# Two transformer blocks on one core: the first layer's modulation by single tiles of features

## The chip, the cores and the metric

The kernel runs as one program on one core of a Trainium2 chip, in float32. The metric is the device time of one launch in microseconds (us), the median of several runs. TensorE (PE in the profile) multiplies matrices; its weight loads have a row of their own (PEld). VectorE (DVE), ScalarE (ACT) and GpSimd (POOL) do the elementwise work, and SyncE (SP) issues the transfers. Each engine works through its own list in order, and waits on semaphores for the others.

## The reference

Two blocks one after the other; 256 latent tokens `x` and 256 context tokens `ctx`, 1024 features. The change lies in the head of the first block's first layer: the modulation and the norm ahead of the first projections.

```python
def first_block(x, c, ctx, c_ctx, w_ada, b_ada, g_norm, w_in, ...):
    silu_c = jax.nn.silu(c)
    silu_cc = jax.nn.silu(c_ctx)
    for l in range(DEPTH):
        mod_lat = silu_c @ w_ada[l] + b_ada[l]
        mod_ctx = silu_cc @ w_ada[l] + b_ada[l]
        x, ctx = _layer(x, ctx, mod_lat, mod_ctx, ...)
    return _rms_norm(x, g_final)
```

In `_layer` the modulation is cut into shift, scale and gate (1024 each). The layer's input is rms_norm(x) * g_norm * (1 + scale) + shift, with one shift and scale for the latent and one for the context tokens, and `w_in` projects it to queries, keys, values and gates. A second layer, and a second block of attention and feed-forward layers, follow.

## The kernel before

Features lie on the 128 partitions: `x[:, k, :]` is tile k of 8, with 512 tokens along it (latent, then context). Products of float32 data are made of three products in the matmul's own rounded format: data and weights are each split into a high part (a cast, on ACT) and a low part (the difference, on DVE or POOL), and `mm` is called for high x high, low x high and high x low. `w_split` splits a piece of weights of 128 x 1024.

The head of layer 0 (`first_layer` with `l == 0`, lines 359 to 426) runs like this. SP loads `x` in four transfers, then for q = 0 to 3 four pieces of `w_ada` (512 columns of shift and scale, that is two tiles of features with their four rows each) and one piece of `w_in_t1`, the weights of the first projection, two tiles of features in a piece. Every transfer here is 512 KB. `Squares` sums the squares of `x` over the features: seven tiles are added up, the columns of that sum and of the last tile's squares are taken by small matmuls (line 100, `tr<-ones,t`), and `rstd` makes the row statistic (`sqm`, then `rcx` by a power on POOL, line 287).

The rest is written as steps, whose order is the string `PLAN["start"]`; `issue_after` keeps each step behind the last matmul so far, and a scheduler sets the final order on each engine from its own estimates of times.

- `d`: one piece of `w_ada` into the sums of the modulation (`ada_mm`, line 184). The sum over 1024 is cut into four quarters, each in its own 32 columns of the array; a piece holds two of the eight k.
- `s`, `b`: the statistic, and its broadcast to all partitions (`rb`, named `tg` in the trace); then all eight tiles of `x` are multiplied by it in place, four on DVE and four on POOL (line 401, `xres`).
- `l`: the modulation of two tiles of features (`ada_rows`): the sums are copied out (line 196, `adarows`), transposed, added up over the quarters on DVE (line 201) with bias and gain (202, 205); then `normed` for both tiles: scale and shift on ACT (line 338), the high part `xyh` (340) and the low part `xyl` (341) on DVE.
- `w`: the split of a piece of `w_in_t1`, the low part on POOL (the table `POOL_LO` holds all four of `t01`).
- `t`: 6 products of one tile of 128 tokens with the two tiles of features of a piece (tiles of PSUM `pv` and `sc`).

Behind it come chunk 3 of the projections (`w_in_t3`, 96 products into `acc` and `sc`), chunk 0, and the attention, which has the steps `d04` and `d05` among its own: the gates' part of the modulation, eight pieces of `w_ada` that are loaded into the four buffers `st`.

Of the kernel before, what the change touches and what calls it, by code (L numbers as in the profile page):

```python
# [10 lines left out]
F32 = mybir.dt.float32  # L11
# [17 lines left out]
def _cols(*spans):  # L29
# [10 lines left out]
# shift 8, scale 8, gate 8  # L40
# [4 lines left out]
# orders of the steps whose results meet only at the end (see the tables `steps`)  # L45
PLAN = {
# [10 lines left out]
# pieces of weights whose low parts are worked out by GpSimd (see the keys given to `fetch`)  # L57
# [5 lines left out]
# tile 0, 1: latent tokens; 2, 3: context tokens  # L63
# [5 lines left out]
def tile_two_blocks(ctx: ExitStack, tc: tile.TileContext, A, out, dbg=None):  # L69
# [104 lines left out]
    # ------------------------------------------------------------------ first block  # L174
# [33 lines left out]
    def ada_src(l, j, i):  # L208
        return A["w_ada"][l, j, :, i * 1024:(i + 1) * 1024]
# [7 lines left out]
    bada = const("b_ada")       # [128, l, 24]  # L217
    gnorm = const("g_norm")
    c2 = const("cvec")
# [28 lines left out]
    class Squares:  # L248
        """sum over the features of squares, a tile of 128 features at a time; a column of sums for each tile of tokens"""
# [14 lines left out]
        def add(self, ap, scale=1.0):  # L264
# [10 lines left out]
            if self.k == KT - 1:        # all but the last tile: ahead of it  # L275
# [4 lines left out]
        def mean(self, dst):  # L280
            """mean of the squares + eps"""
# [8 lines left out]
    def inv_rows(rr, cols):  # L290
        """columns of heads -> rows of 1 / x, a pair of heads in the two halves of the partitions, a pair after the other"""
# [14 lines left out]
    mod_rows = {}       # what is left of the next layer's shifts, scales and gates, and behind which tile  # L306

    def first_layer(l, ncx, x, rc):
        """ncx: context tokens are updated (layer 0) or only read (layer 1)"""
# [8 lines left out]
        # ---- norm  # L318
# [8 lines left out]
        def normed(k, t, r=None):  # L327
            xf = T2()
            if r is not None:
                t1, t = t, T2()  # L330
            # the first tile by halves: the products wait for it
            for hs in (((1,), (0,)) if l and k == 0 else ((0, 1),)):
                s = slice(hs[0] * 256, hs[-1] * 256 + 256)
                if r is not None:
                    V.tensor_tensor(t[:, s], t1[:, s], r[:, s], op=OP.mult)
# [20 lines left out]
        if l == 0:  # L356
# [32 lines left out]
            def st_d(i):  # L389
                q, i = divmod(i, 4)  # L390
                if i == 0:
                    acc[q] = bank("acc")
# [1087 lines left out]
```

## Time and profile before

| | |
|---|---|
| median of 3 runs | 1162.22 us (1160.79, 1162.22, 1164.43) |
| span of the profiled execution | 1164.8 us |
| PE busy over the span | 1110.9 us, 95% |
| DVE, ACT, POOL busy | 765.8, 596.9, 311.7 us |
| HBM read | 164.41 MB, 142 GB/s over the span |

The profiled execution's only time is its span, from the first instruction to the last; it lies 2.6 us above the median and 0.4 above the highest run. A matmul's end is modelled in the trace, so PE's durations overlap; what a matmul costs is read from the distance between two starts. Float32 matmuls (line 100 with `s` or `ones`, line 156) leave two records each, the others one. A timeline row gives the start, the duration, engine and line, what is written from what, the count, and in brackets the engine's idle time ahead of it and what ended that.

### The profile page before, as it was taken

To read this page: it belongs to the slowest core of one execution; us is meant where nothing else is said; L and a number is where in the kernel's file an instruction comes from. 1 tells how busy PE (TensorE), PEld (TensorE's weight loads), DVE (VectorE), ACT (ScalarE), POOL (GpSimd) and SP (SyncE) were. 2 spreads that over 40 slices of the span, in tenths; PEclk is the share of its full clock that TensorE was granted. 3 is DMA by queue.
4 is the path that set the end of the run, shared out by engine and by line. 5 is a ranking of instruction groups with operands and counts; after the bars stand their busy time and mean duration, and the time that the engine had idled before them with its cause. 6 is when DMAs were issued, how large, how long until landed. Compare 5 with 4: busy or idle time off the path is not lost. (4 is left out here: it accounts for less than half of the span.)

```text
span 1164.8 us, 20350 instructions
## 1 busy us (share of the span) xinstructions
PE 1110.9 (95%) x7762; PEld 963.1 (83%) x7762; DVE 765.8 (66%) x1497; ACT 596.9 (51%) x1154; POOL 311.7 (27%) x290
## 2 busy tenths in 40 slices
PE   5899998999899899998999999999999989999997
PEld 2586777687686789887776899999998789999996
DVE  3465555585646666778676777776557877777653
ACT  3435643533434366465456565555447856555541
POOL 3452311131212544424313312221032241222100
PEclk9999998999899899999999999999999999999998
DMA  9523501433742324214443255555644325555561
GB/s 347 200 66 125 177 28 39 142 130 123 259 153 73 101 91 146 74 69 143 162 153 118 82 175 195 184 183 179 182 145 150 135 71 181 185 183 189 175 186 47
DMA packets 52608, 167.29 MB, mean 144 GB/s; under 512 B 6816, under 2 KB 10400, under 8 KB 52512
## 3 DMA queue, kind: packets, MB, share of 16 engines
q1 hardware_dynamic: 52512, 166.01, 42.8%
q8 instruction: 61, 1.00, 0.3%
q14 instruction: 35, 0.29, 0.1%
HBM read 164.41 MB, written 1.05 MB: 142 GB/s over the span
## 5 line engine op out<-in xcount | busy, mean ns | idle before, releaser
L131 ACT CAST wh<-st 128x1024 fp32r<-128x1024 f32 (+4 forms) x272 | 268.5, 992 | 208.9 <-PE acc L100 116.3
L132 DVE TENSOR_TENSOR wl<-st,wh 128x1024 fp32r<-128x1024 f32 (+4 forms) x207 | 244.5, 1183 | 113.3 <-ACT wh L131 108.9
L132 POOL TENSOR_TENSOR wl<-st,wh 128x1024 fp32r<-128x1024 f32 (+4 forms) x65 | 150.9, 2332 | 285.1 <-ACT wh L131 264.5
L100 PE MATMUL acc<-xyh,wh 128*128 128x512 f32 (+1 forms) x320 | 112.5, 352 | 4.3 <-DVE xres L892 2.3
L100 PE MATMUL acc<-xyl,wh 128*128 128x512 f32 (+1 forms) x320 | 111.5, 351 | 2.6 <-DVE xyl L132 2.6
L100 PE MATMUL acc<-xyh,wl 128*128 128x512 f32 (+1 forms) x320 | 111.4, 349 | 0.0
L100 PE MATMUL acc<-wh,xyh 128*128 128x512 f32 (+1 forms) x256 | 97.6, 382 | 6.4 <-DVE t L474 3.3
L100 PE MATMUL sc<-hh,wl 128*128 128x256 f32 x352 | 99.0, 281 | 0.0
L100 PE MATMUL sc<-hl,wh 128*128 128x256 f32 x352 | 99.0, 281 | 0.0
L100 PE MATMUL acc<-hl,wh 128*128 128x256 f32 x352 | 99.0, 281 | 0.0
L100 PE MATMUL acc<-ah,wh 128*128 128x256 f32 x352 | 99.0, 281 | 0.0
L100 PE MATMUL acc<-al,wh 128*128 128x256 f32 x352 | 99.0, 281 | 0.0
L100 PE MATMUL acc<-ah,wl 128*128 128x256 f32 x352 | 98.9, 281 | 0.0
L100 PE MATMUL sc<-hh,wh 128*128 128x256 f32 x352 | 98.9, 281 | 0.0
L100 PE MATMUL acc<-hh,wh 128*128 128x256 f32 x352 | 98.8, 281 | 0.0
L100 PE MATMUL acc<-hh,wl 128*128 128x256 f32 x352 | 98.8, 281 | 0.0
L100 PE MATMUL acc<-wh,xyl 128*128 128x512 f32 (+1 forms) x256 | 96.0, 375 | 0.0
L100 PE MATMUL acc<-wl,xyh 128*128 128x512 f32 (+1 forms) x256 | 95.3, 376 | 0.0
L100 PEld LDWEIGHTS acc<-xyh,wh 128*128 128x128 f32 x320 | 62.2, 194 | 13.5 <-issue 2.8
L100 PEld LDWEIGHTS acc<-xyl,wh 128*128 128x128 f32 x320 | 62.0, 194 | 10.8 <-DVE xyl L132 3.1
L100 PEld LDWEIGHTS acc<-xyh,wl 128*128 128x128 f32 x320 | 62.0, 194 | 7.6
L100 PEld LDWEIGHTS sc<-hl,wh 128*128 128x128 f32 x352 | 66.4, 189 | 0.0
(458 smaller groups left out, 2746.2 us busy)
## 6 DMA issues: line engine op xcount, KB each, us to landing
st<-w_gu SPq DMA_DIRECT2D x88, 512.0 KB, 3.8
st<-w_dn SPq DMA_DIRECT2D x32, 512.0 KB, 3.5
st<-w_in_t SPq DMA_DIRECT2D x24, 512.0 KB, 3.9
st<-w_in_f SPq DMA_DIRECT2D x24, 512.0 KB, 4.7
st<-a_w_qkv SPq DMA_DIRECT2D x24, 512.0 KB, 3.4
st<-w_ada SPq DMA_DIRECT2D x20, 512.0 KB, 3.9
st<-w_out SPq DMA_DIRECT2D x16, 512.0 KB, 4.4
st<-w_dn SPq DMA_DIRECT2D x16, 384.0 KB, 3.3
```

Source lines behind the costliest of these rows:

```text
L100: last_mm[0] = PE.matmul(o, lhsT, rhs, start=start, stop=stop).ins
L131: S.copy(hi, src)
L132: (lo_eng or V).tensor_tensor(lo, src, hi.bitcast(F32), op=OP.subtract)
```

## The change

The modulation of shift and scale is worked out a tile of features at a time. On the host the weights of shift and scale of layer 0 become an array of their own, `w_ada0`, one block of 256 columns (scale and shift of one tile) for each tile. Its two halves of 512 KB are loaded in the order tile 0, piece 0 of `w_in_t1`, tiles 1 and 2, piece 1, tiles 3 and 4, and so on; bytes and number of transfers stay the same. `st_d` makes the sums of one tile: in each half it runs the four quarters side by side, with 256 columns. `st_b` only broadcasts the statistic; the eight multiplications of `x` in place are gone, and the statistic is applied in `st_l` together with the gain: `u = x * gm * rb` (DVE, line 427), the high part as `u + shift` rounded by ACT (428), the low part as `(u + shift) - high` (DVE, 429), in halves of 256 tokens, context first. `bada1` (the bias plus one) is made at the start on POOL. All four splits of `w_in_t1` go to DVE. `st_t` takes one tile of features with all four tiles of tokens, 12 products. The order of steps is new: the column sums and the statistic stand first, and the modulation of the next tile stands ahead of a tile's products.

```diff
-    "start": "d s d d d w b d d d l d l d t t t d w t t d d d l t d d w t t t d t l t t w t t t t",
+    "start": "s d0 b l0 d1 w0 l1 d2 t0 l2 d3 w1 t1 l3 d4 t2 l4 d5 w2 t3 l5 d6 t4 l6 d7 w3 t5 l7 t6 t7",
...
+    bada1 = consts.tile([128, 8], F32, name="bada1")
+    G.tensor_scalar(bada1.rearrange("p (a b) -> p a b", b=2),
+                    bada[:, 0, 0:16].rearrange("p (a b) -> p a b", b=4)[:, :, 0:2], 1.0, None, op0=OP.add)
...
             for q in range(4):
-                tiles = ada_tiles(q)
-                for i, t in enumerate(tiles):
-                    with after(last_load[0]):
-                        load(t, ada_src(0, q, i))
-                wa.append(tiles)
-                with after(last_load[0]):
-                    w1.append(w_load(A["w_in_t1"][0, :, q * n1:(q + 1) * n1]))
+                load_a(2 * q)
+                load_w(q)
+                load_a(2 * q + 1)
...
-            def st_d(i):
-                q, i = divmod(i, 4)
-                if i == 0:
-                    acc[q] = bank("acc")
-                ada_mm(acc[q], i, wa[q][i])
+            def st_d(k):
+                ps = acc[k] = bank("acc")
+                for i in range(2):
+                    for u in range(4):
+                        r = slice(u * 32, u * 32 + 32)
+                        mm(ps[r, :256], s32[:, 4 * i + u, :], wa[k][i][:, u * 256:(u + 1) * 256], i == 0, i == 1)
...
             def st_b():
-                S.copy(rb, bcast4(acc["r"]))
-                for k in range(KT):
-                    (V if k < 4 else G).tensor_tensor(x[:, k, :], x[:, k, :], rb, op=OP.mult)
-
-            def st_l(q):
-                ada_rows(0, q, acc[q])
-                for k in (2 * q, 2 * q + 1):
-                    normed(k, x[:, k, :])
+                pb = bcast4(acc["r"])
+                S.copy(rb, pb)
+
+            def st_l(k):
+                rows = consts.tile([128, 512], F32, name="adarows", bufs=1)[:, :256]
+                S.copy(rows, acc[k][:, :256])
...
+                V.reduce_sum(m, pt[:, :256].rearrange("p (i u r) -> p i r u", u=4, r=32)[:, :, 0:2, :], axis=AX.X)
+                V.tensor_scalar(gm[:, k, :], mod[:, ks, :], bada1[:, k:k + 1], gnorm[:, l, k:k + 1], op0=OP.add, op1=OP.mult)
...
+                for i in (1, 0):
+                    c = slice(i * 256, i * 256 + 256)
+                    V.scalar_tensor_tensor(u[:, c], x[:, k, c], gm[:, k, i:i + 1], rb[:, c], op0=OP.mult, op1=OP.mult)
+                    S.activation(xnh[:, k, c], u[:, c], AF.Identity, bias=sh[:, i:i + 1])
+                    V.scalar_tensor_tensor(xnl[:, k, c], u[:, c], sh[:, i:i + 1], xnh[:, k, c].bitcast(F32),
+                                           op0=OP.add, op1=OP.subtract)
 
             def st_w(q):
-                w1[q] = w_split(w1[q], str(q) in POOL_LO.get("t01", ""))
+                w1[q] = w_split(w1[q], False)
```

On TensorE, from the statistic to the first product of the projections (`pv` from `xyh`), before the change (`kh` holds a piece of `w_ada` here, `wh_217` a split piece of `w_in_t1`):

```order
L156 MATMUL tr_221<-c_ident_64,rcx_203 128x128 x4
L100 MATMUL acc_235<-wh_123,s32_84 32x512 x2
L100 MATMUL acc_235<-wl_124,s32_84 32x512 x2
L100 MATMUL acc_235<-wh_125,s32_84 32x512 x2
L156 MATMUL tr_244<-c_ident_64,adarows_242 128x128 x4
L100 MATMUL acc_235<-wl_126,s32_84 32x512 x2
L156 MATMUL tr_266<-c_ident_64,adarows_264 128x128 x4
L100 MATMUL acc_284<-kh_133,s32_84 32x512 x2
L100 MATMUL pv_287<-wh_217,xyh_108 128x512
```

and with the change, from the column sums on:

```order
L100 MATMUL tr_192<-ones_66,t2_172 128x2 x4
L100 MATMUL tr_192<-ones_66,t2_199 128x2 x4
L100 MATMUL acc_210<-wh_115,s32_86 32x256 x4
L100 MATMUL acc_210<-wl_116,s32_86 32x256 x4
L100 MATMUL acc_240<-wh_117,s32_86 32x256 x4
L100 MATMUL acc_240<-wl_118,s32_86 32x256 x4
L156 MATMUL tr_219<-c_ident_64,rcx_202 128x128 x4
L156 MATMUL tr_227<-c_ident_64,adarows_225 128x128 x2
L100 MATMUL acc_268<-wh_125,s32_86 32x256 x4
L100 MATMUL acc_268<-wl_126,s32_86 32x256 x4
L156 MATMUL tr_255<-c_ident_64,adarows_253 128x128 x2
L100 MATMUL pv_277<-wh_249,xyh_110 128x512
```

Ahead of the first product there stood the modulation of four tiles (`acc_200` and `acc_235`); now that of three (`acc_210`, `acc_240`, `acc_268`) stands there, and both column sums come first.

On ScalarE, from the first split of weights to the scale and shift of the first tiles, before (`tg` is the broadcast statistic, `st_131` is piece 1 of `w_in_t1`):

```order
L131 CAST wh_217<-st_121 128x1024
L196 COPY adarows_242<-acc_200 128x512
L399 COPY tg_199<-tr_221 128x512
L196 COPY adarows_264<-acc_235 128x512
L338 ACTIVATE t2_252<-xres_94,mod0_80,gm0_81 128x256 x2
L338 ACTIVATE t2_257<-xres_94,mod0_80,gm0_81 128x256 x2
L131 CAST wh_310<-st_131 128x1024
```

and with the change:

```order
L131 CAST wh_249<-st_121 128x1024
L414 COPY adarows_225<-acc_210 128x256
L410 COPY tg_201<-tr_219 128x512
L414 COPY adarows_253<-acc_240 128x256
L131 CAST wh_317<-st_131 128x1024
L428 ACTIVATE xyh_110<-t2_233,mod0_82 128x256 x2
```

The cast of piece 1 has moved ahead of the first tile's activations (line 428); it stood behind those of two tiles (line 338).

On TensorE in the attention, around `d04` and `d05`, before the change (`acc_1113` is `d04`, `acc_1174` is `d05`):

```order
L100 MATMUL acc_1113<-st_1126,s32_84 32x512 x2
L100 MATMUL pv_801<-PT_852,vb_464 64x128
L100 MATMUL pv_801<-PT_840,vb_464 64x128
L100 MATMUL pv_801<-PT_852,vb_464 64x128
...
L156 MATMUL tr_976<-c_ident_64,kx_460 128x128 x2
L100 MATMUL acc_1174<-st_1175,s32_84 32x512 x2
L100 MATMUL sc_1085<-kh_465,qs_1077 128x256
L100 MATMUL sc_1085<-kl_466,qs_1077 128x256
L100 MATMUL acc_1174<-st_1179,s32_84 32x512 x2
```

and with the change (`acc_1183` and `acc_1244`):

```order
L100 MATMUL acc_1183<-st_1196,s32_86 32x512 x2
L100 MATMUL sc_1124<-kh_535,qs_864 128x256
L100 MATMUL sc_1124<-kl_536,qs_864 128x256
L156 MATMUL tr_955<-c_ident_64,P_953 128x128 x2
L100 MATMUL pv_935<-PT_946,vb_534 64x128
L156 MATMUL tr_1040<-c_ident_64,kx_530 128x128 x2
L100 MATMUL acc_1244<-st_1245,s32_86 32x512 x2
...
L156 MATMUL tr_1102<-c_ident_64,kx_530 128x128 x2
L100 MATMUL acc_1244<-st_1249,s32_86 32x512 x2
```

The first product of `d05` stands nearer to `d04`, and more work stands between its first and its second product.

## Rows read from the trace of the kernel before

**Rows 1.** Stretches: busy time and count per engine, granted clock, DMA share, GB/s.

```profile
0.00:31.90 31.90, 14.86 (x65) 6.43 (x65) 12.79 (x24) 10.52 (x18) 12.00 (x22) 1.00 0.92 352
31.90:62.00 30.10, 29.87 (x125) 19.10 (x126) 13.97 (x19) 12.15 (x19) 16.25 (x13) 0.94 0.50 169
62.00:90.00 28.00, 28.00 (x137) 23.16 (x136) 18.84 (x60) 11.26 (x28) 14.19 (x15) 1.00 0.25 85
...
95.00:100.00 5.00, 5.00 (x43) 5.00 (x43) 1.48 (x5) 2.81 (x9) 0.00 (x0) 1.00 0.00 0
```

**Rows 2.** Timeline of PE, 12 to 46 us: column sums, modulation, first products.

```profile
16.34 1.87 PE L100 MATMUL tr<-ones,t 128*128 128x2 f32 x8
18.14 1.07 PE L100 MATMUL acc<-wl,s 128*32 128x512 f32 x2
...
19.85 1.92 PE L100 MATMUL acc<-wl,s 128*32 128x512 f32 x4
21.70 0.83 PE L156 MATMUL tr<-c_ident,rcx 128*128 128x128 f32 x4
22.45 0.62 PE L100 MATMUL acc<-wh,s 128*32 128x512 f32 x2
...
31.89 0.50 PE L100 MATMUL pv<-wh,xyh 128*128 128x512 f32 x1 [3.57 <-DVE xyh L340]
...
35.76 0.40 PE L100 MATMUL pv<-wl,xyh 128*128 128x512 f32 x1
...
42.17 0.62 PE L100 MATMUL acc<-kx,s 128*32 128x512 f32 x2
...
43.05 1.03 PE L100 MATMUL acc<-qkT,s 128*32 128x512 f32 x4
```

**Rows 3.** Timeline, 18 to 32 us: the chain ahead of the first product.

```profile
18.25 0.16 DVE L282 SCALAR_TENSOR_TENSOR sqm<-tr,sqh 128x4 f32<-128x4 f32 x1 [3.48 <-PE tr L100]
18.56 1.02 POOL L287 TENSOR_TENSOR rcx<-sqm,nhalf 128x4 f32<-128x4 f32 x1 [15.91 <-DVE sqm L282]
...
22.56 0.59 ACT L399 COPY tg<-tr 128x512 f32<-128x512 f32 x1 [0.16 <-PE tr L156]
...
23.18 5.73 DVE L401 TENSOR_TENSOR xres<-xres,tg 128x512 f32<-128x512 f32 x4 [4.77 <-ACT tg L399]
23.23 6.80 POOL L401 TENSOR_TENSOR xres<-xres,tg 128x512 f32<-128x512 f32 x4 [1.33 <-ACT tg L399]
...
28.83 0.18 DVE L201 TENSOR_REDUCE mod<-tr 128x8 f32<-128x32 f32 x1
...
30.28 2.07 ACT L338 ACTIVATE t<-xres,mod,gm 128x256 f32<-128x256 f32 x4 [3.66 <-DVE gm L205]
```

**Rows 4.** Timeline: SP's issues of w_ada, and the cast of the ninth transfer.

```profile
10.91 0.33 SPq L103 DMA_DIRECT2D wh<-w_ada  x1
...
12.18 0.33 SPq L103 DMA_DIRECT2D wl<-w_ada  x1
...
17.32 1.05 ACT L131 CAST wh<-st 128x1024 fp32r<-128x1024 f32 x1 [5.18 <-DMA st<-w_in_t]
```

**Rows 5.** Groups by form on DVE: busy us, mean ns of one, idle before.

```profile
L983 DVE SCALAR_TENSOR_TENSOR hl<-hres,c_g_sec,hh 128x256 fp32r<-128x256 f32 x24 | 18.7, 788 | 4.0 <-ACT hh L982 4.0
L341 DVE TENSOR_TENSOR xyl<-t,xyh 128x512 fp32r<-128x512 f32 x15 | 10.3, 689 | 0.3
...
L652 DVE SCALAR_TENSOR_TENSOR tg<-tg,acc 128x256 f32<-128x256 f32 x4 | 1.7, 414 | 1.7 <-ACT tg L651 1.7
```

**Rows 6.** Timeline, 55 us: a split's low part on DVE.

```profile
55.27 1.23 DVE L132 TENSOR_TENSOR wl<-st,wh 128x1024 fp32r<-128x1024 f32 x1 [3.96 <-ACT wh L131]
```

**Rows 7.** Timeline of PE: the last product of chunk 3, first of chunk 0.

```profile
86.88 0.40 PE L100 MATMUL sc<-wl,xyh 128*128 128x512 f32 x1
87.11 0.29 PE L100 MATMUL acc<-wh,xyh 128*128 128x272 f32 x1
```

**Rows 8.** Timeline of PE in the attention: the second product of `d05`.

```profile
114.75 1.92 PE L100 MATMUL acc<-st,s 128*32 128x512 f32 x4 [2.08 <-DMA st<-w_ada]
```

More of the change, by code (lines that the diff above doesn't have):

```diff
@@ L208, in ada_src @@
     def ada_src(l, j, i):
-        return A["w_ada"][l, j, :, i * 1024:(i + 1) * 1024]
+        return A["w_ada"][j - 4 if l == 0 else 2 + j, :, i * 1024:(i + 1) * 1024]
     def ada(l, j):
@@ L215, in ada @@
         ada_rows(l, j, ps)
+    c2 = const("cvec")
     bada = const("b_ada")
     gnorm = const("g_norm")
-    c2 = const("cvec")
+    bada1 = consts.tile([128, 8], F32, name="bada1")
+    G.tensor_scalar(bada1.rearrange("p (a b) -> p a b", b=2),
+                    bada[:, 0, 0:16].rearrange("p (a b) -> p a b", b=4)[:, :, 0:2], 1.0, None, op0=OP.add)
     for l in range(2):
@@ L325, in first_layer, with normed @@
         xnl = xy.tile([128, KT, 512], F32R, name="xyl")
[L327 to L330, printed above, removed]
+        def normed(k, t1, r):
+            xf, t = T2(), T2()
             for hs in (((1,), (0,)) if l and k == 0 else ((0, 1),)):
                 s = slice(hs[0] * 256, hs[-1] * 256 + 256)
-                if r is not None:
-                    V.tensor_tensor(t[:, s], t1[:, s], r[:, s], op=OP.mult)
+                V.tensor_tensor(t[:, s], t1[:, s], r[:, s], op=OP.mult)
                 for i in hs:
@@ L367, in ada_tiles, with load_a, load_w @@
                         sb.tile([128, 1024], F32, name="vn")]
-            n1 = 2 * len(T_CHUNKS[1])
-            wa, w1 = [], []
-            for q in range(4):
-                tiles = ada_tiles(q)
-                for i, t in enumerate(tiles):
-                    with after(last_load[0]):
-                        load(t, ada_src(0, q, i))
-                wa.append(tiles)
-                with after(last_load[0]):
-                    w1.append(w_load(A["w_in_t1"][0, :, q * n1:(q + 1) * n1]))
+            n1 = len(T_CHUNKS[1])
+            wa, w1 = {}, []
+            def load_a(k):
+                if k % 2 == 0:
+                    tiles = ada_tiles(k // 2)
+                    wa[k], wa[k + 1] = tiles[:2], tiles[2:]
+                for i, t in enumerate(wa[k]):
+                    with after(last_load[0]):
+                        load(t, A["w_ada0"][k, :, i * 1024:(i + 1) * 1024])
+            def load_w(q):
+                with after(last_load[0]):
+                    w1.append(w_load(A["w_in_t1"][0, :, 2 * q * n1:2 * (q + 1) * n1]))
+            for q in range(4):
+                load_a(2 * q)
+                load_w(q)
+                load_a(2 * q + 1)
             with after(last_load[0]):
@@ new lines, in st_b @@
+                S.copy(rb, pb)
+            def st_l(k):
+                rows = consts.tile([128, 512], F32, name="adarows", bufs=1)[:, :256]
+                S.copy(rows, acc[k][:, :256])
+                pt = bank("tr")
+                for i in range(2):
+                    transpose(pt[:, i * 128:(i + 1) * 128], rows[:, i * 128:(i + 1) * 128])
+                ks = k + k // 2 * 2
+                m = mod[:, ks:ks + 3:2, :]
+                V.reduce_sum(m, pt[:, :256].rearrange("p (i u r) -> p i r u", u=4, r=32)[:, :, 0:2, :], axis=AX.X)
+                V.tensor_scalar(gm[:, k, :], mod[:, ks, :], bada1[:, k:k + 1], gnorm[:, l, k:k + 1], op0=OP.add, op1=OP.mult)
+                sh = mod[:, ks + 2, :]
+                V.tensor_scalar(sh, sh, bada[:, l, ks + 2:ks + 3], None, op0=OP.add)
+                u = T2()
+                for i in (1, 0):
[4 more added lines that the diff above has]
+                                           op0=OP.add, op1=OP.subtract)
@@ new lines, in st_w, with st_t @@
+            def st_w(q):
+                w1[q] = w_split(w1[q], False)
+            def st_t(k):
+                hi, lo = w1[k // 2]
+                c = slice(k % 2 * n1, k % 2 * n1 + n1)
+                for i, t in enumerate(order):
+                    if k == 0:
+                        pss1[t] = bank(("pv", "pv", "sc", "sc")[i])
+                    ts = slice(t * 128, t * 128 + 128)
+                    mm(pss1[t], xnh[:, k, ts], hi[:, c], k == 0, False)
+                    mm(pss1[t], xnh[:, k, ts], lo[:, c], False, False)
+                    mm(pss1[t], xnl[:, k, ts], hi[:, c], False, k == KT - 1)
@@ L873, in first_layer @@
             for k in range(8):
-                load(gt[3][k], A["w_ada"][1, 3, :, k * 512:(k + 1) * 512])
+                load(gt[3][k], A["w_ada"][5, :, k * 512:(k + 1) * 512])
             gt[3] = [gt[3][2 * i:2 * i + 2] for i in range(4)]
@@ L1427, in _arrays @@
     a["b_ada"] = i["b_ada"].reshape(2, 24, 128)[:, ADA_TILES].transpose(2, 0, 1)
-    a["w_ada"] = np.stack([_blocks(i["w_ada"][l][:, _cols(*((t * 128, 128) for t in ADA_TILES))], 512) for l in range(2)])
+    wa = [i["w_ada"][l][:, _cols(*((t * 128, 128) for t in ADA_TILES))] for l in range(2)]
+    a["w_ada"] = np.concatenate([_blocks(wa[0], 512)[4:], _blocks(wa[1], 512)])
+    a["w_ada0"] = _blocks(i["w_ada"][0][:, _cols(*((t * 128, 128) for k in range(8) for t in (8 + k, k)))], 256)
     for n, cols in enumerate(T_CHUNKS):
```

13 lines of the change are left out of this document (1 added, 12 removed).

## The prediction

> **What bounds the kernel now.** I read the stretches first. From 31.9 to 90 us PE has no idle time to speak of (29.87 of 30.10 us, then 28.00 of 28.00), and DVE, ACT and POOL are busy for half of it or less [rows 1]. Ahead of 31.9 us PE is busy for 14.86 us, and the DMA engines for 0.92 of the stretch [rows 1]. So two things set the end of the head: when the first product of the projections starts, and what PE has to do from there. Next comes PE's timeline: that product starts at 31.89 us after 3.57 us in which PE waited for `xyh` [rows 2]. What ended late there is the chain on the other engines: the broadcast is copied out at 22.56, then DVE multiplies four tiles of `x` for 5.73 us while POOL does four in 6.80, and only behind that, at 28.83, DVE comes to the modulation and ACT at 30.28 to scale and shift [rows 3]. Chunk 3 ends at 87.11 [rows 7], 55.2 us after the first product.
>
> **The change: the start of the products.** The second block of column sums took from 16.34 to 18.14 [rows 2], and stood behind a piece of the modulation. With the change it follows the first block directly, so it ends at about 16.4. `sqm` needs DVE, where the split of piece 0 now stands ahead of it. SP issues at 10.91 and 12.18, one transfer each 1.28 us, and the ninth transfer (piece 0) landed at 17.32 [rows 4]; piece 0 is now the seventh, at 14.75. Its cast takes 1.05 [rows 4], its low part 1.23 on DVE [rows 6], so `sqm` is at 17.1, not 16.4: that edit costs 0.7 us, and POOL, whose list it leaves, has nothing there. From `sqm` to the end of `rcx` is 1.33 us [rows 3]: 18.4. PE meanwhile does the modulation of tiles 0 and 1. At the low clock two pieces side by side took 1.71 us (18.14 to 19.85) [rows 2], and a tile is two pieces of that size, so PE is at 16.4 + 3.4 = 19.8, later than `rcx`. Broadcast 0.75 (21.70 to 22.45) [rows 2], two transposes half of that: 20.95. The copy of the statistic, 0.59 [rows 3], ends at 21.25; a copy of half a modulation row some 0.4 (0.59 for a whole), 21.6; then comes the cast of piece 1, the twelfth transfer, landed at 21.16: 22.7. Then half of tile 0 on ACT (2.07 / 4 = 0.52 [rows 3]): the first product is at **23.3**. The DVE branch (three small operations of 0.18 [rows 3] and two products of 0.41 [rows 5]) would be there at 22.8, so ACT's cast is what comes last. The move is **8.6 us**; I bound it by 9.1 (the cast hidden) and 7.4 (each of ACT's and PE's handovers later by some tenths).
>
> **From there to the end of chunk 3.** The 192 products stay, at 0.23 us each (86.88 to 87.11) [rows 7]. Three terms differ.
> - The clock. [...] (The granted clock of the stretch to 31.9 reads 1.00 throughout [rows 1]; since the rows at 18.14 take double the time of those at 42.17, I go by durations.) With the change PE goes from 16.4 to 22.9 with no gap of over half a microsecond and meets its first product then. I take the row at 22.45 as the nearer one: **2.0 us** gained; the other end is nothing.
> - The modulation. Before, seven pieces ran in this stretch, mostly alone; a piece alone lasts 1.03 (at 43.05), hardly less than two side by side [rows 2]. Now ten run in pairs, 5 x 0.9 = 4.5 against some 6, but in 12 transposes for 8 and more switches, some 1 us back. I take **0.5** gained, between 0.9 and a loss of 0.6.
> - The pace of the other engines. PE needs 12 x 0.23 + 0.9 + 0.3 = 4.0 us for a tile. DVE needs three small operations (0.55), four halves at 0.41 to 0.48, half a split (0.62), and a wait of 0.2 for ACT between `u` and the low part: 3.2. ACT needs 0.4 + 1.04 + 0.52 = 2.0. So the tiles' work is hidden under PE's products; only for tile 0 does the split of piece 1 stand ahead of `xyl`, and I charge **0.4** for it. Transfers don't bind: tile 7's second half is the 24th, at 36.5, where PE comes to it after 43.
>
> The multiplications of `x` (5.73 on DVE, 6.80 on POOL [rows 3]) go from the path, and what is late next is ACT's cast, as above. Moving the small constants costs nothing: `cvec` comes earlier, and `bada1` runs on a POOL that is idle.
>
> [...] Rows first: 512 columns take 0.689 on DVE, 256 take 0.414 [rows 5], so two halves cost 0.14 more than a whole, 16 such pairs 2.2 us. [...]
>
> **Behind the head.** The scheduler also moved work in the attention. The second product of `d05` waited 2.08 us for its weights [rows 8]; those loads wait until `d04` has read the buffers. Now the first product of `d05` stands some 2 us of work nearer to `d04` and the second farther off. The wait is shared out anew; I charge **0.5**, between 2 us lost and 1.5 gained.
>
> **Sum.** -8.6 - 2.0 - 0.5 + 0.4 + 0.5 = -10.2. The profiled execution has 1164.8, 2.6 above the median of 1162.22; the sum is a difference, so I take it off the median: **1152.0**.
>
> **The rivals.**
> 1. DVE sets the pace. The dearest halves of this kind in the trace take 0.788 [rows 5], beside a busy POOL; four of those make 0.55 + 3.15 + 0.62 + 0.3 = 4.6 a tile, 0.6 over PE's 4.0, and 7 x 0.6 = 4.2 us come back. Then 1156.2. For it: low parts stand behind splits in DVE's list. Against: POOL has nearly nothing in the head now.
> 2. The head's gain is swallowed behind it: the loads for the attention set their own time, and PE waits there for as long as it came early. Then 1162. For it: the wait of 2.08 us [rows 8]. Against: from 95 to 100 us the DMA engines move nothing [rows 1], so those loads wait for PE and shift with it.
> [...]
> 4. The order isn't what the change says, and the first product waits for more than the cast of piece 1: were transfers later by 0.2 us each, the twelfth would land 2.4 later, 1154.4; it lies in the range.
>
> **How the numbers follow.** A measurement of this kernel can tell 0.3%, 3.5 us. The forecast (with rival 4) has 0.77, rival 1 0.12, rival 2 0.07, rival 3 0.04. The forecast's own ends: the start by -0.5 and +1.2, the clock by +2.0, PE's work by -0.4 and +1.1, behind the head by -2 and +1.5; not all at once, so -3.0 and +2.5, 1149.0 to 1154.5. To hold 8 in 10 the range takes in rival 1: **1149.0 to 1157.0**. Faster by over 0.3%: the forecast and nearly all of rival 1, 0.88. Same: rival 2 and a remainder, 0.08. Slower: 0.04.
>
> **What would show it.** The first `pv` product at 23 to 24 us, with ACT's cast of piece 1 just ahead of it; products 0.23 apart from the start (the clock term) or 0.43 for the first eight; tiles 4.0 us apart with no waits for `xyl` over half a microsecond (rival 1 if they are 4.6 apart); chunk 3's last product at 76 to 77 us; the stretch behind shifted as a whole. It would be wrong if PE's waits ahead of 85 us sum to more than 2 us, or if the wait at `d05` grows by as much as the head won.

## The result and the profile after

The changed kernel takes 1150.53 us (median of 4 runs, 1149.4 to 1151.07) beside 1162.24 for the kernel before (4 runs, 1160.79 to 1164.43): a ratio of 0.9899, 95% interval 0.9885 to 0.9913, 11.7 us less. Forecast were 1152.0 us, 10.2 less. In a later series, with 11 runs of before (median 1160.75) and 4 of after (1150.21), the difference is 10.5 us. The size came out; two terms of the sum did not, and they cancel, as shown below.

The profiled execution of after has a span of 1148.8 us and took 1150.56. That of before (span 1164.8) took some 4 us more than its median; so the comparison goes by a second trace of before as well, taken among the experiments (span 1159.9).

PE's timeline of after at the start (start, us, engine, line, operation, out<-in, count, idle before and what ended it):

```profile
18.40 1.08 PE L100 MATMUL acc<-wh,s 128*32 128x256 f32 x8
19.26 0.95 PE L100 MATMUL acc<-wl,s 128*32 128x256 f32 x8
...
20.94 0.64 PE L100 MATMUL acc<-wh,s 128*32 128x256 f32 x8
21.39 0.61 PE L100 MATMUL acc<-wl,s 128*32 128x256 f32 x8
...
23.63 0.50 PE L100 MATMUL pv<-wh,xyh 128*128 128x512 f32 x1 [1.25 <-ACT xyh L428]
23.96 0.40 PE L100 MATMUL pv<-wl,xyh 128*128 128x512 f32 x1
24.20 0.39 PE L100 MATMUL pv<-wh,xyh 128*128 128x512 f32 x1
...
```

And what ACT does ahead of that product:

```profile
21.31 0.38 ACT L414 COPY adarows<-acc 128x256 f32<-128x256 f32 x1
22.12 1.04 ACT L131 CAST wh<-st 128x1024 fp32r<-128x1024 f32 x1 [0.43 <-DMA st<-w_in_t]
23.07 0.91 ACT L428 ACTIVATE xyh<-t,mod 128x256 fp32r<-128x256 f32 x2
```

The first product stands at 23.63 and not at 31.89 as in [rows 2]; PE waits 1.25 us for `xyh`, not 3.57, and what came late is ACT's cast of piece 1, as the prediction named it. The second product follows the first after 0.33 us and the others after 0.23, where the first eight of before took 3.87 us. Four sums of the modulation (x8, two records each) take 0.86 us to the next at 18.40 and 0.45 at 20.94: their pace has nearly doubled ahead of the products. (The granted clock reads 1.00 in both places, from 18.40 to 20.90 and from 20.90 to 23.60.)

The stretch of after that answers to the second of [rows 1] (us, PE, PEld, DVE, ACT, POOL busy and count, granted clock, DMA share, GB/s):

```profile
31.90:62.00 30.10, 29.38 (x157) 20.25 (x157) 21.93 (x42) 13.71 (x31) 12.59 (x13) 1.00 0.58 198
```

And where chunk 3 ends and chunk 0 begins, in after:

```profile
79.02 0.39 PE L100 MATMUL sc<-wl,xyh 128*128 128x512 f32 x1
79.24 0.28 PE L100 MATMUL acc<-wh,xyh 128*128 128x272 f32 x1
```

Chunk 0 begins at 79.24 instead of 87.11 [rows 7]: 7.9 us earlier, 0.4 less than the first product won, though 2.0 more were forecast for the clock. So the stretch in between lost more than 2 us of its own. And some 4 us of the 11.7 (2.6 of the 10.5) are not in the head at all.

A table of marks, all read from PE's timelines (start of the first product, start of chunk 0, span), for the runs below:

| kernel | first product | chunk 0 | between | span | median us |
|---|---|---|---|---|---|
| before, first trace | 31.89 | 87.11 | 55.2 | 1164.8 | 1162.2 |
| before, second trace | 31.77 | 86.99 | 55.2 | 1159.9 | 1160 to 1161 |
| after | 23.63 | 79.24 | 55.6 | 1148.8 | 1150.5 |
| after, second trace | 23.52 | 79.13 | 55.6 | 1149.4 | 1150.2 |
| statistic only | 29.22 | 89.89 | 60.7 | 1158.4 | 1162.4 |
| multiplied in place | 30.76 | 87.62 | 56.9 | 1156.6 | 1157.4 |
| transposes tied | 24.65 | 76.84 | 52.2 | 1146.5 | 1147.0 |
| sums before rows | 22.53 | 74.83 | 52.3 | 1140.8 | 1146.0 |
| low parts on POOL | 23.64 | 80.80 | 57.2 | 1153.8 | 1151.3 |
| before, shifted | 31.41 | 85.69 | 54.3 | 1153.9 | 1156.0 |
| before, only `xyh`, `xyl` shifted | 32.72 | 87.35 | 54.6 | 1153.9 | 1156.8 |
| after, shifted back | 23.34 | 79.52 | 56.2 | 1152.0 | 1152.8 |

A span is one execution; single executions of one kernel differ by up to some 3 us either way, so verdicts go by the ratios below and places by the marks. The head as a whole starts up to 1.1 us earlier or later from one execution to the next (the first column sum at 12.34 to 13.48), which moves both marks together.

### The profile page after: what moved, and what is told of

The parts are those of the page before. It is cut to its first block, busy times and chain, and to the rows that moved or that the text cites. A ratio compares the mean times of both kernels' runs of the same rounds, so it can differ in the third digit from the quotient of the medians.

```text
span 1148.8 us, 20497 instructions
## 1 busy us (share of the span) xinstructions
PE 1096.8 (95%) x7826; PEld 960.6 (84%) x7826; DVE 772.9 (67%) x1525; ACT 596.6 (52%) x1158; POOL 295.6 (26%) x283
## 3 DMA queue, kind: packets, MB, share of 16 engines
q8 instruction: 62, 1.02, 0.3%
## 5 line engine op out<-in xcount | busy, mean ns | idle before, releaser
L132 DVE TENSOR_TENSOR wl<-st,wh 128x1024 fp32r<-128x1024 f32 (+4 forms) x211 | 250.0, 1187 | 110.6 <-ACT wh L131 106.2
L132 POOL TENSOR_TENSOR wl<-st,wh 128x1024 fp32r<-128x1024 f32 (+4 forms) x61 | 140.7, 2317 | 272.3 <-ACT wh L131 246.3
```

The costliest lines, as they stand in the source:

```text
L132: (lo_eng or V).tensor_tensor(lo, src, hi.bitcast(F32), op=OP.subtract)
```

## The experiments

**A second trace of before.**

> The kernel before, unchanged, for a second trace. The traced execution of before has a span of 1164.8 us, which is some 4 us above what the median of its times (1162.2, less 1.8 around the span) allows, and in it the granted clock fell to 0.73 from 115 to 120 us. If that execution had lost its 4 us in the attention by chance, a second trace has a span near 1160.5, the first product of the projections again at 31.9, chunk 3's end again at 87.1, d05's first product near 110.8, and the 4 us less only behind that. If the order of before makes the loss there every time, the second trace shows d05's last product again near 120.5, and the 4 us are lost elsewhere.

The span is 1159.9, and up to 105 us every mark is 0.12 us from the first trace. Then they part: the second product of `d05` starts at 112.48 with no wait for its weights, where it waited 2.08 us in [rows 8], and `d05`'s last products at 117.09 instead of 120.49. The granted clock of 95 to 130 us is 1.00 here and 0.95 there. So 3.4 us of the first trace were that execution's own. The wait itself was not: in the two shifted versions of before (below), whose orders are those of before, the second product of `d05` waits 0.98 and 1.02 us for its weights. PE's timelines, of this trace and of before shifted:

```profile
112.48 1.05 PE L100 MATMUL acc<-st,s 128*32 128x512 f32 x4
```

```profile
112.20 1.05 PE L100 MATMUL acc<-st,s 128*32 128x512 f32 x4 [0.98 <-DMA st<-w_ada]
```

In after the wait stands ahead of the first product of `d05` instead (1.64 us in its second trace), and the second has none:

```profile
103.18 1.05 PE L100 MATMUL acc<-st,s 128*32 128x512 f32 x4 [1.21 <-DMA st<-w_ada]
```

**One part alone: the statistic applied with the norm.**

> Before, with one part of the change alone: x is no longer multiplied by the row statistic in place; each tile is multiplied when it is normed. Theory 1 (the multiplications in place are the largest piece of what the start waits for): the chain ahead of the first product loses 5.7 us on DVE and gets 0.7 back for the tile's own multiplication, so the first product moves from 31.9 to 26.5 to 27.5, and 4 to 6 us come off the whole: 1156 to 1158. Theory 2 (the column sums and the transfers of the modulation hold the start, so that the fused multiplication without the new order gives little): the first product stays at 30 or later, and the time within 2 us of before. Theory 3 (DVE, with eight multiplications more inside the projections, sets their pace): the start moves but chunk 3's end does not.

```diff
             S.copy(rb, bcast4(acc["r"]))
-            for k in range(KT):
-                (V if k < 4 else G).tensor_tensor(x[:, k, :], x[:, k, :], rb, op=OP.mult)
...
-                    normed(k, x[:, k, :])
+                    normed(k, x[:, k, :], rb)
```

1162.42 us, 1.0009 of before (0.9993 to 1.0025): nothing. The first product moves to 29.22, by half of what I had thought, and chunk 0 comes 2.9 us later than in before. DVE's and POOL's timelines in this run:

```profile
29.93 2.73 DVE L335 TENSOR_TENSOR t<-xres,tg 128x512 f32<-128x512 f32 x1
...
35.19 2.59 DVE L340 CAST xyh<-t 128x512 fp32r<-128x512 f32 x1
```

```profile
29.22 2.90 POOL L132 TENSOR_TENSOR wl<-st,wh 128x1024 fp32r<-128x1024 f32 x1 [7.68 <-ACT wh L131]
34.87 2.63 POOL L132 TENSOR_TENSOR wl<-st,wh 128x1024 fp32r<-128x1024 f32 x1 [2.75 <-ACT wh L131]
```

And PE's:

```profile
33.06 0.50 PE L100 MATMUL pv<-wh,xyh 128*128 128x512 f32 x1 [2.38 <-DVE xyh L340]
33.78 0.63 PE L100 MATMUL pv<-wh,xyl 128*128 128x512 f32 x1 [0.22 <-DVE xyl L341]
34.21 0.63 PE L100 MATMUL pv<-wl,xyh 128*128 128x512 f32 x1
```

The multiplication takes 2.73 us instead of 0.69 while POOL works out a low part; the cast behind it comes late, PE waits 2.38 us for it and then runs its products 0.43 apart (33.78 to 34.21). A cast that falls beside POOL's next low part takes 2.59 us instead of 0.42. Theory 3 holds: with steps of two tiles, whole tiles on DVE and POOL busy beside it, DVE sets the pace. This part alone is worth nothing. (What it would be worth with the low parts moved to DVE, but the old order, was not run.)

**One part undone: the multiplications back in place.**

> After, with one part undone: the eight multiplications of x by the row statistic are back in place, four on DVE and four on POOL, ahead of tile 0. Theory 1: DVE's four take 5.7 us behind the copied statistic, and the first product moves from 23.6 to between 28.5 and 29.5; PE does one or two pieces of the modulation in the gap, so 4 to 6 us of it are left at chunk 3's end, and the whole is 1154 to 1157. If the clock term was real too, the first products are again 0.4 to 0.5 apart behind the idle stretch instead of 0.23, which would be part of it. Theory 2 (the order of the loads and sums made the gain): the whole stays within 2 us of 1150.5.

```diff
                 S.copy(rb, pb)
+                for k in range(KT):
+                    (V if k < 4 else G).tensor_tensor(x[:, k, :], x[:, k, :], rb, op=OP.mult)
...
-                    V.scalar_tensor_tensor(u[:, c], x[:, k, c], gm[:, k, i:i + 1], rb[:, c], op0=OP.mult, op1=OP.mult)
+                    V.tensor_scalar(u[:, c], x[:, k, c], gm[:, k, i:i + 1], None, op0=OP.mult)
```

1157.44 us, 0.9966 of before (0.9954 to 0.9978), some 7 above after. That it is under before at all is not the order's doing: its operands have after's place, which alone is worth as much (see the place of the operands). DVE, then PE:

```profile
21.71 5.71 DVE L412 TENSOR_TENSOR xres<-xres,tg 128x512 f32<-128x512 f32 x4
27.34 1.22 DVE L423 TENSOR_SCALAR gm<-mod,bada,c_g_norm 128x2 f32<-128x2 f32 x1
...
28.69 1.21 DVE L132 TENSOR_TENSOR wl<-st,wh 128x1024 fp32r<-128x1024 f32 x1
```

```profile
30.76 0.80 PE L100 MATMUL pv<-wh,xyh 128*128 128x512 f32 x1 [8.01 <-ACT xyh L430]
31.35 0.63 PE L100 MATMUL pv<-wl,xyh 128*128 128x512 f32 x1
31.78 0.63 PE L100 MATMUL pv<-wh,xyh 128*128 128x512 f32 x1
...
37.13 0.39 PE L100 MATMUL pv<-wl,xyh 128*128 128x512 f32 x1
37.36 0.40 PE L100 MATMUL pv<-wh,xyl 128*128 128x512 f32 x1
```

The four multiplications (5.71 us), a small operation that takes 1.22 us and ends with POOL's four (28.56 beside 28.53), and the low part of piece 1 (1.21 us), which now stands ahead of tile 0's norm, put the first product at 30.76, 1.3 later than expected. PE stands idle for 8.01 us, and the twelve products of tile 0 run some 0.4 apart, against 0.23 for the next tile's: 35.49 less 30.76 is 4.7 us where 12 x 0.23 would be 2.8. So the 2 us that the forecast puts down to the clock come back here, behind a wait of 8.01 us; behind the 1.25 us of after the products stand 0.23 apart. Theory 1 holds, and the gap costs more than it said, since PE fills little of it: with the new order of loads and sums, but the multiplications in place, the head ends 0.5 to 0.6 later than in before. Neither part alone brings anything; together they bring 7.8 us there.

**The transposes tied ahead of the next sums.**

> After, with the next piece of the modulation issued only behind the transposes of the tile before, so that they no longer cut the eight products of a half into groups of six and two. Theory 1 (the cut and its two extra changeovers are why a tile took 4.5 to 4.9 us instead of 4.0): the tiles come 4.2 to 4.5 us apart, chunk 3 ends 1.5 to 2.5 us earlier than 79.2, at 76.7 to 77.7, and the whole loses 1 to 2.5 us: 1148 to 1149.5. Theory 2 (the transposes and the modulation cost the same wherever they stand): the tiles stay 4.5 to 4.9 apart, no difference. Theory 3 (what comes early is given back in the attention): chunk 3 ends earlier by 1.5 or more, and the whole is the same within 0.5 us. Rival on the other side: PE now waits for ACT's copy of the row ahead of each transpose, 0.3 to 0.5 a tile, and the whole is 1 to 3 us longer.

```diff
                     transpose(pt[:, i * 128:(i + 1) * 128], rows[:, i * 128:(i + 1) * 128])
+                last_mm[0] = last_tr[0]
```

First what after does between two tiles, PE's timeline from tile 1 to tile 2:

```profile
30.73 0.64 PE L100 MATMUL acc<-kh,s 128*32 128x256 f32 x8
31.19 0.61 PE L100 MATMUL acc<-kl,s 128*32 128x256 f32 x6
31.73 0.44 PE L156 MATMUL tr<-c_ident,adarows 128*128 128x128 f32 x2
32.10 0.62 PE L100 MATMUL acc<-kl,s 128*32 128x256 f32 x2
32.65 0.50 PE L100 MATMUL pv<-wh,xyh 128*128 128x512 f32 x1
```

And the same place with the transposes tied:

```profile
31.67 0.38 PE L156 MATMUL tr<-c_ident,adarows 128*128 128x128 f32 x2
31.98 0.64 PE L100 MATMUL acc<-kh,s 128*32 128x256 f32 x8
32.44 0.61 PE L100 MATMUL acc<-kl,s 128*32 128x256 f32 x8
32.98 0.50 PE L100 MATMUL pv<-wh,xyh 128*128 128x512 f32 x1
```

In after the scheduler put the two transposes among the eight sums of a tile, ahead of the last one (the trace counts each sum as two, so 8, 6 and 2): 1.92 us from 30.73 to 32.65. Tied, transposes and sums take 1.31 (31.67 to 32.98). Tiles come 4.16 or 4.17 us apart, each of the five, where in after they come 4.16, 4.86, 4.46, 4.88 and 4.87 apart: 4.16 where the transposes stand ahead of all sums, 4.46 where they stand between the two halves, 4.86 to 4.88 ahead of the last sum. The wait of 0.7 us for `xyl` that after has at tile 7 is gone too. Chunk 0 starts at 76.84, 2.4 earlier though the first product was 1.0 later: 52.2 us instead of 55.6. Of these 3.4, 2.0 lie in the sums and transposes between the products of the projections: from start to start they take 7.2 us here, 9.2 in after and 7.3 in before. Another 0.9 is tile 7's wait. The whole takes 1146.96, 0.9872 of before (0.9851 to 0.9894). Theory 1 holds, with more than it promised.

**Tile 2's sums ahead of tile 1's transposes, on top of that.**

> The version with the transposes tied, and tile 2's column sums moved ahead of tile 1's transposes, so that TensorE has work while ACT copies tile 1's row (there it waited 0.87 us at 23.3, and the first product came at 24.65). Theory: the first product at 23.5 to 24.0, chunk 3's end at 75.7 to 76.3 instead of 76.8, and the whole 0.5 to 1.2 us less: 1146 beside 1147. Rival: the first product's operand comes from ACT at 23.5 to 24 and is late next, so that no more than 0.3 us are left. A third: the attention takes it back, the head's end earlier and the time the same.

```diff
-    "start": "s d0 b l0 d1 w0 l1 d2 t0 l2 d3 w1 t1 l3 d4 t2 l4 d5 w2 t3 l5 d6 t4 l6 d7 w3 t5 l7 t6 t7",
+    "start": "s d0 b l0 d1 w0 d2 l1 t0 l2 d3 w1 t1 l3 d4 t2 l4 d5 w2 t3 l5 d6 t4 l6 d7 w3 t5 l7 t6 t7",
```

PE's timeline ahead of the first product:

```profile
22.33 0.44 PE L156 MATMUL tr<-c_ident,adarows 128*128 128x128 f32 x2 [0.24 <-ACT adarows L414]
22.53 0.48 PE L100 MATMUL pv<-wh,xyh 128*128 128x512 f32 x1
```

PE waits 0.24 us instead of 0.87, and the first product is at 22.53 with nothing to wait for; chunk 0 starts at 74.83, 12.2 us before that of before. (1.1 of the 2.1 us at the first product, and of the 2.0 at chunk 0, are the execution's own: tile 0's sums ran at 16.30 here and at 17.43 with the transposes only tied.) 1146.03 us, 0.9871 of before (0.9845 to 0.9897): the best of these kernels, though from the version with the transposes only tied the times can't tell it.

**The low parts left on POOL.**

> After, with the low parts of pieces 1 to 3 worked out by POOL, as part of them was before, and not by DVE. DVE has 1.23 us less for every two tiles, and POOL is busy for 2.4 to 2.8 us for each piece. In before, DVE's casts took 1.83 and 2.61 us instead of 0.42 while POOL worked out such a piece. Theory 1 (rival 1 of the prediction, that DVE beside a busy POOL sets the pace, would have come true with POOL at work): DVE's halves beside POOL take 0.8 or more, TensorE waits for xyh or xyl for 1 us or more in some tiles, chunk 3 ends 1 to 3 us later than 79.2, and the whole is 1 to 3 us longer. Theory 2 (TensorE is so far from waiting for DVE that it does not matter): chunk 3 within 0.4 us of 79.2, or earlier by some tenths. Behind the head the scheduler moves more, so the head is read from the trace.

```diff
-                w1[q] = w_split(w1[q], False)
+                w1[q] = w_split(w1[q], q > 0)
```

1151.30 us, 0.9924 of before (0.9898 to 0.9950), which the times can't tell from after; the head ends 1.6 us later than in after, at 80.80. It is lost at tile 0, where PE waits 0.49 and 0.46 us for halves of `xyl`: its products take 4.36 us instead of 2.85. DVE and POOL:

```profile
23.32 2.35 DVE L421 TENSOR_SCALAR gm<-mod,bada,c_g_norm 128x2 f32<-128x2 f32 x1
```

```profile
23.26 2.39 POOL L132 TENSOR_TENSOR wl<-st,wh 128x1024 fp32r<-128x1024 f32 x1 [4.64 <-ACT wh L131]
```

POOL's low part runs from 23.26 to 25.65, and a DVE operation on 2 columns that begins at 23.32 ends with it, at 25.67. It takes 0.29 at 28.63, in the next tile. The two ends are 0.02 us apart; why the one lasts as long as the other, no row shows. So what rival 1 feared was there, a DVE operation of 2.35 us beside a busy POOL; what mostly kept it away is that the change also took POOL's low parts out of the head.

**The place of the operands.** The three next runs are about the 4 us that came behind the head. In the traces of before the products of 512 columns with `xyh` and `xyl` stand 0.233 us apart, in those of after 0.227 to 0.231 (means by stretch), and so also where the granted clock is 1.00 in both. (The expectations below put the end of this at 400 us; the traces show it again between 500 and 640, as said behind them.) The change brings a small tile, `bada1`, 32 bytes a partition, and all that is allocated behind it lies 32 bytes lower: `xyh` at 172160, a multiple of 64, and not at 172192. (These places follow from the order of allocation; no trace shows an address.)

> Before with nothing but one unused tile of 32 bytes a partition behind g_norm, the size that bada1 has in the change. The order of every engine stays word for word (POOL clears the tile once more), but all that is allocated behind it, the projections' operands xyh and xyl among it, lies 32 bytes lower in each partition: xyh begins at 172160, a multiple of 64, as in after, and not at 172192. In the traces the products of 512 columns stand 0.2333 us apart in before and 0.228 to 0.230 in after, up to 400 us; behind that, where both programs have the same addresses, they agree. Theory 1 (the place of the operands makes the difference, and with it some 3.5 of the 11.7 us): the spacing falls to 0.228 to 0.230, the head ends where it did (87.0 less some 0.5 to 1), and the whole loses 3 to 4.5 us: 1156.5 to 1158 beside 1161. Theory 2 (the new order of chunk 0 and the attention, or chance, made those us): the spacing stays at 0.233 and the time within 1 us of before.

```diff
     gnorm = const("g_norm")
+    G.memset(consts.tile([128, 8], F32, name="pad"), 0.0)
```

> Before, with unused tiles of 32 bytes placed so that of the tiles of the first layer only xyh and xyl change their place against multiples of 64 bytes (172192 to 172160, 188576 to 188544); xres and the L0 tiles keep theirs. No engine's order changes but POOL's, which clears the unused tiles. Theory 1 (the operands of the projections are what matters): the spacing of the 512-column products is 0.228 to 0.230, and the time is that of the version with everything shifted, 1155 to 1157.5. Theory 2 (another of the shifted tiles, such as the copies and temporaries that DVE and ACT write meanwhile, made it): spacing 0.233, and the time within 1.5 us of 1161. In between, 0.231: both.

```diff
         xnl = xy.tile([128, KT, 512], F32R, name="xyl")
+        if l == 0:
+            G.memset(xy.tile([128, 8], F32, name="padx"), 0.0)
...
             steps[f_[0]](*map(int, f_[1:]))
+        G.memset(sb.tile([128, 8], F32, name="pads"), 0.0)
         yh, yl = y
```

> After with bada1 made 64 bytes wide instead of 32 (half of it unused), every engine's order unchanged: xyh begins at 172128, again not a multiple of 64. Theory 1 (place of the operands): the spacing of the products goes back to 0.233 in the first 400 us, and 3 to 4.5 us come back: 1153.5 to 1155 beside 1150.5; what is left against before is the head's 7.75. Theory 2 (order or chance): no change, within 1 us of 1150.5.

```diff
-    bada1 = consts.tile([128, 8], F32, name="bada1")
+    bada1 = consts.tile([128, 16], F32, name="bada1")[:, 0:8]
```

One stretch at the end of layer 0 in which PE does nothing but products of 512 columns with `xyh` and `xyl`, 316 to 338 us (length, PE's busy time and count of matmuls, the same of PEld, DVE, ACT and POOL, clock, DMA share, GB/s). Before (second trace):

```profile
316.00:338.00 22.00, 22.00 (x96) 17.69 (x95) 10.10 (x15) 6.33 (x8) 2.41 (x1) 1.00 0.56 171
```

Before, shifted:

```profile
316.00:338.00 22.00, 22.00 (x99) 18.23 (x98) 10.86 (x17) 6.58 (x8) 0.00 (x0) 1.00 0.56 165
```

Before, only `xyh` and `xyl` shifted:

```profile
316.00:338.00 22.00, 22.00 (x99) 18.22 (x98) 11.54 (x18) 7.23 (x9) 1.84 (x1) 1.00 0.51 159
```

After:

```profile
316.00:338.00 22.00, 22.00 (x98) 18.21 (x98) 11.78 (x16) 7.13 (x9) 2.40 (x1) 1.00 0.45 154
```

After, shifted back:

```profile
316.00:338.00 22.00, 22.00 (x96) 17.73 (x95) 11.40 (x18) 7.08 (x9) 1.53 (x1) 1.00 0.52 152
```

In the same 22 us, with PE always busy at a granted clock of 1.00, 96 products go through where `xyh` begins at an odd multiple of 32, and 98 or 99 where it begins at a multiple of 64. More closely, PE's timeline over a row of 144 such products, the first and the last. In before (second trace):

```profile
315.48 0.39 PE L100 MATMUL acc<-xyh,wh 128*128 128x512 f32 x1
...
348.84 0.39 PE L100 MATMUL acc<-xyl,wh 128*128 128x512 f32 x1
```

In after:

```profile
306.74 0.40 PE L100 MATMUL acc<-xyh,wh 128*128 128x512 f32 x1
...
339.16 0.39 PE L100 MATMUL acc<-xyl,wh 128*128 128x512 f32 x1
```

33.36 us against 32.42 for 143 distances: 0.2333 and 0.2267. Farther on, over a row of 28, first in before (second trace):

```profile
560.58 0.48 PE L100 MATMUL acc<-wl,xyh 128*128 128x512 f32 x1
...
566.96 0.40 PE L100 MATMUL acc<-wl,xyh 128*128 128x512 f32 x1
```

and in after:

```profile
550.54 0.48 PE L100 MATMUL acc<-wl,xyh 128*128 128x512 f32 x1
...
556.78 0.39 PE L100 MATMUL acc<-wl,xyh 128*128 128x512 f32 x1
```

6.38 us against 6.24, with a longer first step in both. All thirteen traces fall into two groups by the place alone. In the four with the place of before or one shifted back (before twice, the statistic only, after shifted back) the mean distance is 0.233 both up to 400 us and from 500 to 640; in the nine others it is 0.2284 to 0.2289. At some 0.0047 each, the 1248 products of this kind are worth 5.9 us.

Products of fewer columns with the same two tiles do not follow. Those of 272 columns stand 0.125 to 0.126 apart in all traces. Those of 256 go the other way: 33 in a row last 3.74 us from the first to the last in before (second trace, from 444.57) and 3.83 in after (from 433.40), that is 0.117 and 0.120; over some 490 of them about 1 us is given back.

The times: before shifted 1155.97, 0.9958 of before (0.9943 to 0.9973), though every engine's order is that of before (POOL clears one tile more); with only `xyh` and `xyl` shifted 1156.83, 0.9972 (0.9961 to 0.9983); after shifted back 1152.80, 0.9935 (0.9916 to 0.9955), 2.6 us above after in the same series (1150.21, 0.9912), with intervals that overlap. By the distances theory 1 holds three times over. By the medians 4.8, 3.4 and 2.6 us hang on the place of those two tiles, with the order of instructions unchanged; the first and the last of these times are 0.5 and 0.7 us below the ranges expected.

**The rest of the operands.**

> The version with the transposes tied, and unused tiles of 32 bytes so that the operands of the later stages (hh, hl, ah, al, moh, mol, cqh, ckh) also begin at multiples of 64; orders unchanged. Theory 1, carried further (operands that start at an odd multiple of 32 cost every product a few nanoseconds, whatever its width): the 256-column products of the later stages, 0.118 us apart now, come to 0.115 to 0.116; there are some 3500 of them, so 5 to 10 us come off: 1137 to 1142 beside 1147. Theory 2 (only the 512-column products of the first layers, or only the place of one operand against another, are concerned): the spacing behind 400 us stays at 0.118 and the time within 1.5 us of 1147. Against theory 1 stands that loh and lol began at multiples of 64 all along, and their spacing is 0.12 as well.

```diff
     gqn = const("g_lora")
+    G.memset(consts.tile([128, 8], F32, name="pad"), 0.0)
...
                 self.hg = hp.tile([128, KT, 256], F32, name="hg", bufs=1)
+                G.memset(hp.tile([128, 8], F32, name="padh", bufs=1), 0.0)
...
         r2 = sb.tile([128, 2], F32, name="lr2")
+        G.memset(sb.tile([128, 8], F32, name="padm"), 0.0)
```

1148.89 us, 0.9891 of before (0.9872 to 0.9910), no better than the 1146.96 of the same orders without it (0.9872 of before; it is 0.4 above the range expected, but the intervals overlap). The products of 256 columns behind 640 us stay 0.118 to 0.119 apart. Theory 2 holds: the effect is not one of every operand. Which of the two tiles it needs, and why products of 512 columns alone gain by it, was not tried and stays open.

**After again.**

> The changed kernel itself, for a second trace and for times beside the three above. By all theories 1150 to 1151.5; head's end again at 79.2, spacing of the 512-column products 0.228 to 0.230.

1150.21 us, chunk 0 at 79.13, distances of 0.227 to 0.231 in the stretches up to 400 us: as expected.

## Why the prediction came out, point by point

- **The start of the products: right.** Forecast 8.6, measured 8.1 to 8.3 (31.77 and 31.89 to 23.63). ACT's cast of piece 1 was last, as foreseen; it stood at 22.12 and not at 21.6, since it waited 0.43 us for its transfer, which came 0.9 later than the 21.16 reckoned.
- **The clock: right in size.** Forecast 2.0, a term that no run shows by itself. What the traces show in its place: the first eight products take 3.87 us in before, 0.23 of it a wait for `xyl`, at a granted clock of 0.58, and 1.94 in after (23.63 to 25.57), at 1.00. That is 1.9 us. Behind waits of 3.57 us (before), 2.38 (statistic only) and 8.01 (multiplied in place) the products stand 0.43 apart at first; behind the 1.25 of after they stand 0.23 apart from the second on. The granted clock does not tell all of it: it reads 1.00 in before from 18.14 to 21.70 and from 22.45 to 24.30, though two pieces of sums take 1.71 us at 18.14 and 0.89 at 22.45. The stretches (us, PE, PEld, DVE, ACT, POOL busy and count, granted clock, DMA share, GB/s), in before, then in after:

```profile
31.90:36.00 4.10, 3.87 (x9) 2.80 (x10) 3.37 (x5) 4.10 (x7) 2.49 (x1) 0.58 1.03 392
```

```profile
23.60:25.60 2.00, 1.97 (x9) 1.64 (x10) 2.00 (x6) 0.63 (x2) 0.00 (x0) 1.00 1.05 420
```

- **The modulation: the term that was mis-sized.** Forecast 0.5 gained, and 0.4 lost for `xyl` of tile 0, for which PE did not wait. From the first product to chunk 0, before takes 55.2 us and after, shifted back so that the products' own pace is that of before, 56.2. With 2.0 won by the clock, that stretch has lost 3.0 us of its own instead of winning 0.1. Of these, 1.9 are the sums and transposes between the products (7.3 us in before, 9.2 in after), 0.65 the wait for `xyl` of tile 7, and about 0.4 the longer step (0.33 us instead of 0.23) at each of four switches more. The failing step is "12 x 0.23 + 0.9 + 0.3 = 4.0 us for a tile", and with it the pairs at 0.9 of the modulation's term: both took it that a tile's eight sums stay together. The scheduler put the transposes among them, and four tiles of five took 4.46 to 4.88. Tied, it takes 4.16, and the sums and transposes take 7.2. The order of the changed program shows that without any run (seven sums, the transposes, one sum); the prediction gave no price to the two changeovers more.
- **The pace of DVE: right up to tile 6.** In after DVE waits 0.56 to 1.97 us for PE's transposes ahead of its reductions for tiles 3 to 6, and in these tiles PE waits for nothing of DVE's. The halves cost 0.44 each (0.88 for two in after), as counted. So the 2.2 us that the halves cost more by [rows 5], for which the sum has no term, reach PE in none of these tiles: DVE has the time to spare. At tile 7 rival 1 shows: POOL works out low parts again from 50.17 on, two operations of DVE on 2 columns take 2.16 and 2.44 us, a half of `xyl` 2.30 instead of 0.44, and PE waits, some 0.9 us lost in all. "POOL has nearly nothing in the head" held up to there only; of 31.9 to 62 us POOL is busy for 12.59. POOL, DVE and PE in after:

```profile
56.98 2.39 POOL L132 TENSOR_TENSOR wl<-st,wh 128x1024 fp32r<-128x1024 f32 x1 [1.98 <-ACT wh L131]
```

```profile
57.34 2.30 DVE L429 SCALAR_TENSOR_TENSOR xyl<-t,mod,xyh 128x256 fp32r<-128x256 f32 x1 [0.86 <-ACT xyh L428]
```

```profile
59.70 0.50 PE L100 MATMUL sc<-wh,xyl 128*128 128x512 f32 x1 [0.72 <-DVE xyl L429]
```

- **Behind the head: the mechanism was there, the size can't be told.** Forecast 0.5 lost. As forecast, the wait of `d05` moved from its second product to its first: 1.2 to 1.6 us there in three traces, where before has 0 to 2.1 us ahead of the second. From chunk 0's start to the first products of the gates (121.05 in the second trace of before, 113.85 in after) before takes 34.1 and after 34.6; but before shifted takes 35.1, after's second trace 35.0 and after shifted back 36.6, so single traces differ by more than the term.
- **What the forecast lacked: the place of the operands.** 2.6 to 4.8 us, 0.6 to 0.9 of it in the head (56.2 against 55.6, and 55.2 against 54.3) and the rest up to 640 us. No part of the prediction looked at addresses.

So the sum would have read -8.2 - 2.0 + 3.0 + 0.5 = -6.7, and with the place of the operands, 2.6 to 4.8 us, -9.3 to -11.5; measured are 11.7, and 10.5 in the later series. The head alone, with the operands put back, is worth 8.0 by the times (1160.75 to 1152.80; interval 5.2 to 9.8). That the forecast of 10.2 lay near is partly luck: a term of 3.0 of the wrong sign and one of some 4 that was not seen. Of the signs that the prediction named, the first product at 23 to 24 us and the distance of 0.23 came; tiles 4.0 us apart and chunk 3's last product at 76 to 77 did not (it stands at 79.02). Of the tail behind 130 us the traces can't tell every microsecond, since single executions differ there by some 3 us.

Of the rivals, the first was there at tile 7 (DVE operations of 2.16 to 2.44 us beside POOL's low parts), and ahead of it was kept off by taking POOL's low parts out of the head. The second (swallowed by the loads) did not come. Nor did the third, with the tiles' products 0.43 apart: in after they stand 0.23 apart, and the granted clock of 31.9 to 62 us is 1.00. The fourth came in part: the twelfth transfer was 0.9 us late, of which 0.5 reached the cast.

## What to carry to other kernels

Two parts of a change can each be worth nothing and together be worth the most: ask what would be late next after each, and run them apart. Where a new order comes out of a scheduler, price the groups as they stand in it, not as they are written; two transposes among eight sums cost 0.3 to 0.7 us a tile. And where a change adds or removes even a small tile, compare the addresses of the matmuls' operands ahead of and behind it, or a layout effect will pass for one of the order.

## What the runs showed of the hardware that was not expected

- A product of 512 columns with `xyh` or `xyl`, in the matmul's own format, takes 0.233 us from one to the next, or 0.227 to 0.231, by whether these two tiles begin at an odd multiple of 32 bytes or at a multiple of 64 (96 against 98 or 99 matmuls in 22 us at a clock of 1.00). Products of 272 columns with the same tiles showed no such thing (0.125 to 0.126), and those of 256 the reverse (0.117 in before, 0.120 in after).
- A DVE operation on 2 columns took 2.35 us instead of 0.29, as long as POOL's operation beside it ran (with the low parts left on POOL).
- With two transposes among a tile's sums, the way from the first sum to the next product took 1.92 us; with the transposes ahead of them all, sums and transposes together took 1.31.
